# Order of steps in two gate pairs of an encoder block, and the place of the FFN operand's splits

## The chip, the cores and the metric

The kernel runs on one core of a Trainium2 chip. The metric is device time in microseconds (us) from the first to the last instruction of a launch with its overhead, as the median of several runs. The engines of the core work side by side, each on its own list of instructions: TensorE (PE; PEld is its weight load), VectorE (DVE), ScalarE (ACT), GpSimd (POOL) and SyncE (SP), which issues most of the DMAs.

## The reference

One encoder block on 256 tokens of width 2048, all in float32: a projection of the normalised input, three attention mixers, a gated merge of their outputs, an output projection with a residual, and a SwiGLU channel mixer with a residual. What matters here is the part after the mixers:

```python
gates = jax.nn.sigmoid(gt.astype(jnp.float32)).reshape(b, s, N_BRANCH, D_MODEL)
merged = (gates[:, :, 0] * (oa @ w_br_a[layer]).astype(jnp.float32)
          + gates[:, :, 1] * (ob @ w_br_b[layer]).astype(jnp.float32)
          + gates[:, :, 2] * (oc @ w_br_c[layer]).astype(jnp.float32)).astype(x.dtype)
x = x + merged @ w_o[layer]

hf = rms_norm(x, g_ffn[layer]) @ w_ffn_in[layer]
x = x + (jax.nn.silu(hf[..., :D_FF]) * hf[..., D_FF:]) @ w_ffn_out[layer]
```

`gt` are the 6144 gate columns of the first projection, so each gate is a product of the normalised input with a 2048 x 2048 block of weights.

## The kernel before, in words

**Products in halves.** Weights stream from HBM in blocks of 256 rows by 512 columns, held as a tile of 128 x 1024 floats. A float32 product is made of three products of a shorter float format: every operand is written as a high half `hi` plus a low remainder `lo`, and hi·hi, hi·lo and lo·hi are summed in PSUM. For a block of weights, ScalarE copies it to `whi` (L452) and VectorE subtracts that from the block to get `wlo` (L463). For the tokens' side the same is done once for each operand by `split` (L130): ScalarE makes the high half, VectorE the low one. The tokens' side has to lie with its channels on the partitions, so a result of one stage is transposed by TensorE against the identity into a PSUM tile `tp` and then split into the operand of the next stage: `transposed` (L303).

**Pairs and steps.** From the gated merge to the end, the work is a list of *pairs*, each of them two column blocks (c = 0 and c = 1) of 512. `pair` (L465) turns strings of step names into functions. An ordinary step, `d4` or `D4`, is one block of weights for column block 0 or 1: 12 matmuls of 512 columns. The other letters are the seven products with which a 2 x 2 arrangement of blocks is multiplied in place of eight: `X W Y P Z Q H`, each with 6 matmuls. Of them `P`, `Q` and `H` first need a sum or a difference of two weight blocks, which VectorE forms in place (L653, L655, L657) ahead of the split. `S1` to `S4` do the same for a block of one unit: 6 matmuls for each of the first three, two half-size splits, and a half-size sum (L584 to L590). `l0`, `l1`, `r0`, `r1` and `s0` only issue loads. A dot is a free place: it takes the next step of the *tail* of the pair before, that is, ordinary steps that this pair left over.

**What sets the order.** TensorE and SyncE keep the order in which the program was written. On ScalarE and VectorE the order is that of a scheduler with a simulated time line, except for instructions handed to `follow` (L93): each of these is tied behind the last one so handed on its engine, and together they form the sequence of halves. `run` (L690) writes them: it makes a step ready (its in-place sum, if it has one, then its `whi`), then the `wlo` of the step before (`low(1)`), and then emits the products of the step that is four behind (`ahead`), so

```python
            products = ready()
            if products is None:
                continue
            low(1)
            waiting.append(products)
            if len(waiting) > ahead:
                waiting.pop(0)()
                tick()
```

There are five pairs of buffers for `whi` and `wlo` (four in `wp` and, at every fifth step, one in `more`), so a step's `whi` can only be written when the products of the step five before it have been read. What follows a finished column block (sigmoids L975, multiplications L989, additions L995 and L1047, transposes, splits) is written by small side jobs; `tick` lets them go on, and a job that yields n goes on n emitted steps later. These jobs are not in the sequence of halves, but have a high priority with the scheduler.

**Where the change works.** `merging` (L962) runs five gate pairs, numbered by `nth` from 0. Pair 1 takes `STEPS_GATE5` (L57), pair 2 `STEPS_GATE52` (L58). The tail that pair 1 finds is d7, then D0 and d0 of the first branch product; that of pair 2 is d5, d6, d7 of pair 1. In pair 4 the merged block 0 is transposed for the output projection: its job adds the gated products to `mg` (L995), yields 4, and transposes (L1002 to L1006). `projecting` (L1026) makes the output projection in two pairs; each finished block is added to the residual `x` (L1047), squared, transposed and split, scaled by the gain of the FFN's norm, into `x1T` (L1062), the operand of the FFN. In `transposed` a block of 512 columns is done in two halves, each with four transposes and two splits; for `x1T` the second half stood two steps after the first.

Of the kernel before, what the change touches and what calls it, by code (L numbers as in the profile page):

```python
# [11 lines left out]
F32 = mybir.dt.float32  # L12
# [3 lines left out]
ALU = mybir.AluOpType  # L16
# [3 lines left out]
S = 256  # L20
# [33 lines left out]
STEPS_GATE = [  # L54
    ("l0 l1 X0 X1 r0 W0 r1 W1 d4 P0 P1 d5 Y0 Y1 Q0 Q1 Z0 Z1 d6", "D4 H0 D5 H1 D6 D7", "d7"),
    ("l0 l1 X0 X1 . r0 W0 r1 W1 P0 P1 . Y0 Y1 . Q0 Q1 .", "Z0 Z1 D4 H0 D5 H1 D6 D7", "d4 d5 d6 d7")]
STEPS_GATE5 = ("l0 l1 s0 X0 . . X1 S1 r0 W0 r1 W1 P0 P1 S2 . Y0 Y1 Q0 Q1 S3", "Z0 Z1 D5 H0 D6 H1 D7 S4", "d5 d6 d7")  # L57
STEPS_GATE52 = ("l0 l1 s0 X0 . X1 S1 r0 W0 r1 W1 . P0 P1 S2 . Y0 Y1 Q0 Q1 S3",) + STEPS_GATE5[1:]  # L58
STEPS_O = ("l0 s0 X0 S1 . r0 W0 . P0 S2 Y0 . Q0 S3 .", "Z0 D3 H0 D6 S4 d3 D7 d6 D4 D5", "d7 d4 d5")
STEPS_O2 = ("l0 s0 X0 S1 r0 W0 . P0 S2 Y0 . Q0 S3 .", "Z0 D3 H0 D4 S4 d3 D5 D6 D7", "d4 d5 d6 d7")  # L60
STEPS_FFN0 = ("l0 l1 X0 X1 . r0 W0 . r1 W1 . P0 P1 . Y0 Q0 Q1 Y1", "Z0 Z1 D6 H0 D7 H1 D4 D5", "d6 d7 d4 d5")
# [43 lines left out]
def encoder_block(ctx: ExitStack, tc: tile.TileContext, a: dict, out: bass.AP):  # L105
# [21 lines left out]
        return psum.tile([P, NC], F32, name=name, tag=tag, bufs=2 if tag in ("c1", "tp") else 4)  # L127


    def split(hi, lo, src, scale=None):  # L130

        if scale is None:
            nc.scalar.activation(hi, src, AF.Copy)  # L133
            nc.vector.tensor_sub(lo, src, hi.bitcast(F32))  # L134
        else:
            nc.scalar.activation(hi, src, AF.Copy, scale=scale)
            nc.vector.scalar_tensor_tensor(lo, src, scale, hi.bitcast(F32), op0=ALU.mult, op1=ALU.subtract)

    def root_of(v, shape, to):

# [159 lines left out]
            pass  # L300
        known.add(name)

    def transposed(src, dst, g=None, lag=1, also=None, single=None):  # L303


        full = None
        for h in range(2):
            if h:
                yield lag
            tp = bank("tp", "tp")  # L310
            for k in range(2):
                for t in range(T):
                    nc.tensor.transpose(tp[:, k * S + t * P:k * S + (t + 1) * P],
                                        src[t][:, (2 * h + k) * P:(2 * h + k + 1) * P], ident)
            if g is None:
                d = dst(2 * h, 2)
                split(d[0], d[1], tp.rearrange("p (k s) -> p k s", s=S))
            else:
                for k in range(2):
                    d = dst(2 * h + k, 1)  # L320
                    split(d[0], d[1], tp[:, k * S:(k + 1) * S], g(2 * h + k))
            if also is not None:
                if full is None:
                    full = s4([P, 2, 4, P], "ffull")
                to, of = full[:, :, 2 * h:2 * h + 2], tp.rearrange("p (k t s) -> p k t s", t=T, s=P)
                if g is None:
                    nc.scalar.activation(to, of, AF.Copy)
                else:
                    for k in range(2):
                        nc.scalar.activation(to[:, k], of[:, k], AF.Copy, scale=g(2 * h + k))  # L330
            if single is not None and h == 0:
                one = s4([P, 1, 4, P], "ffull")
                nc.scalar.activation(one[:, 0], tp.rearrange("p (k s) -> p k s", s=P), AF.Copy)
                start(urgent(token_sums_later(one, single)))
        if also is not None:
            token_sums(full, also)
# [625 lines left out]
    def merging():  # L962
        nth = 0
        start(lone_of_gates())
        parts = [s8([P, 2, PK, NC], "both", F32, tail) for _ in range(2)]
        extra = [(Part(r[:, i]), f"gate{2 * n + i}") for n, r in enumerate(parts) for i in range(2)]
        free.extend(extra)
        for b, (g0, k0, k1) in enumerate(((0, 0, 2), (8, 2, 6), (4, 6, 12))):
            for j in (0, 2) if b else (2,):
                sg, br = {}, {}  # L970

                def gates(c, r, j=j, b=b, sg=sg, br=br):
                    sg[c] = s4([P, T, NC], "sg")
                    for t in range(T):
                        nc.scalar.activation(sg[c][:, t], r[t], AF.Sigmoid, scale=r_x[:, 0, t:t + 1])  # L975
                    if c in br:
                        merge(c, [br[c][:, t] for t in range(T)], j, b, sg)

                def branch(c, r, j=j, b=b, sg=sg, br=br):
                    if c in sg:  # L980
                        return merge(c, r, j, b, sg)
                    br[c] = s4([P, T, NC], "br")
                    for t in range(T):
                        nc.scalar.activation(br[c][:, t], r[t], AF.Copy)

                def merge(c, r, j, b, sg):
                    n0 = (j + c) * NC
                    for t in range(T):
                        nc.vector.tensor_mul(sg[c][:, t] if b else mg[t][:, n0:n0 + NC], r[t], sg[c][:, t])  # L989

                    def later():
                        yield 1
                        for t in range(T):
                            m = mg[t][:, n0:n0 + NC]
                            nc.vector.tensor_add(m, m, sg[c][:, t])  # L995
                        if b == 2:
                            to = mT[j + c] = s8([P, 2, 4, S], "mT", pool=home(j + c))
                            if j + c == 0:
                                room.extend(form_room(1))
                            if j + c == 1:  # L1000
                                lone["w_o"] = s4([P, 1, 2, 4, P], "lone", F32R)
                            yield 2 if j + c == 2 else 4  # L1002
                            yield from transposed([mg[t][:, n0:n0 + NC] for t in range(T)],
                                                  lambda k, n: (to[:, 0, k:k + n], to[:, 1, k:k + n]),
                                                  lag=2, also=room[0] if j + c == 0 else None,
                                                  single=lone["w_o"] if j + c == 1 else None)  # L1006
                    if b:
                        start(urgent(later()))

                if nth == 3:  # L1010
                    retired.extend(extra)
                    free[:] = [f for f in free if f not in extra]
                front, back, end = pair(block_pair(a["w_gate"], g0 + j), xT,
                                        STEPS_GATE52 if nth == 2 else STEPS_GATE5 if nth == 1 else STEPS_GATE[min(nth, 1)], gates, TWO,
                                        by_room(lambda: gforms), early=nth == 0, fresh="Y" if nth < 2 else "",
                                        single=(4, of_lone("gate")))
                n = (k1 - k0) // 2
                of_br = pair(lambda u, c, j=j, k0=k0: a["w_br"][j + c][k0 // PK + u], lambda k, k0=k0: ol(k0 + k),
                             ("", " ".join(o + str(u) for o in ("dD" if nth else "Dd") for u in range(n)), ""), branch)[1]
                yield (front, back + of_br, end) if nth else (front, back, end + of_br)  # L1020
                nth += 1
# [4 lines left out]
    def projecting():  # L1026
# [16 lines left out]
        for n in (0, 2):  # L1043
            def add(c, r, n=n):
                xc = [x[t][:, (n + c) * NC:(n + c + 1) * NC] for t in range(T)]
                for t in range(T):
                    nc.vector.tensor_add(xc[t], r[t], xc[t])  # L1047
                ended.append(n + c)
                last = len(ended) == 4

                def later():
                    yield 1
                    sq = s4([P, T, NC], "sq")
                    for t in range(T):
                        nc.scalar.activation(sq[:, t], xc[t], AF.Square, accum_out=ss1[:, t, n + c:n + c + 1])
                    if last:
                        start(urgent(root()))
                    yield 2
                    if not x1T:
                        x1T.extend(s8([P, 2, 4, S], "x1T") for _ in range(4))  # L1060
                        room.extend(form_room(3))
                    yield from transposed(xc, lambda k, m: (x1T[n + c][:, 0, k], x1T[n + c][:, 1, k]),  # L1062
                                          lambda k: gT[:, 2, 4 * (n + c) + k:4 * (n + c) + k + 1], 2,
                                          also=room[2 + n + c] if n == 0 else None)
                start(urgent(later()))
            yield pair(block_pair(a["w_o"], n), mTl, STEPS_O2 if n else STEPS_O, add, TWO[:1], by_room(lambda: room),
                       single=(2, of_lone("w_o")))
# [139 lines left out]
```

## Time and profile before

| | |
|---|---|
| median of 3 runs | 1360.47 us (1360.01 to 1360.65) |
| the profiled execution | 1360.15 us, of it 1358.4 us from the first to the last instruction |
| granted TensorE clock | 1.000 |
| TensorE, VectorE, ScalarE busy | 99%, 87%, 64% of the span |
| matmuls and transposes | 6160 |
| moved by DMA | 301.19 MB, 222 GB/s |
| gate pairs 1 and 2 | about 351 to 404 and 404 to 456 us |
| output projection | about 571 to 678 us |

In the time line a row is a run of instructions of one kind: start, duration, engine, line, operation, output and inputs, shape, count, and in brackets the idle time of the engine just before it with what ended it. `raw`, `more` and `both` are the places of loaded weights. `mmX`, `mmW` and so on are the PSUM banks of a pair: X also takes the products `P` and `Q`, W takes `Z` too. `forms` and `glone` are operands of the seven products, `xT`, `oT`, `mT` those of ordinary steps. A busy TensorE isn't TensorE at its peak, since a matmul's end is modelled and overlaps the next one's start: a wait shorter than that overlap shows only in the distance of starts.

### The profile page before, as it was taken

What the parts mean: (1) busy time and instruction counts of PE and PEld (TensorE: products, weight loads), DVE (VectorE), ACT (ScalarE), POOL (GpSimd) and SP (SyncE); (2) the same over time, 40 slices, a digit from 0 to 9 for tenths busy, and PEclk for the clock granted to TensorE, in tenths of its full rate; (3) what the DMA queues carried; (4) which work ended last, traced back from release to release, by engine and by line L of the source; (5) the groups of instructions that cost most, each with busy time, mean ns of one, the idle gap of its engine ahead of it and who ended that gap; (6) DMA issues with size and microseconds to landing.
All of it is one profiled execution on the core that took longest, in us unless ns stands there. A gap on an engine that the chain in (4) does not pass through costs nothing.

```text
span 1358.4 us, 17355 instructions
## 1 busy us (share of the span) xinstructions
PE 1350.5 (99%) x6160; PEld 1118.3 (82%) x6160; DVE 1176.4 (87%) x1458; ACT 864.4 (64%) x1136; POOL 53.1 (4%) x60
## 2 busy tenths in 40 slices
PE   9999999999999999999999999999999999999998
PEld 8888888888887888888888888888888888888887
DVE  6878877768989869788999998988999889989997
ACT  7876665655666656656776666555666655566664
POOL 0010000000000000000000000000000000000000
PEclk9999999999999999999999999999999999999999
DMA  9976455558494594873678666688666786666872
GB/s 368 348 240 210 141 155 181 160 162 288 186 307 144 184 297 154 287 253 118 224 233 263 209 205 215 225 263 262 191 216 215 248 263 209 219 221 210 277 223 98
DMA packets 86344, 301.19 MB, mean 222 GB/s; under 512 B 9777, under 2 KB 12337, under 8 KB 86001
## 3 DMA queue, kind: packets, MB, share of 16 engines
q1 hardware_dynamic: 79488, 275.94, 57.8%
q0 software_dynamic: 6624, 24.12, 9.4%
q8 instruction: 48, 0.79, 0.2%
q14 instruction: 40, 0.32, 0.1%
q10 hardware_dynamic: 144, 0.02, 0.0%
HBM read 297.17 MB, written 2.88 MB: 221 GB/s over the span
## 4 chain that ended last, share of the span: by engine, by line
PE 95%; DVE 3%; ACT 1%; issue 1%; POOL 0%; DVEq 0%; POOLq 0%; ACTq 0%
PE mmX L80 28%; PE mmW L80 20%; PE mm L80 17%; PE mmY L80 15%; PE mmQ L80 11%; DVE wlo L463 2%; PE tp L80 1%; PE sc L80 1%; PE o L80 1%; PE pT L80 1%; PE mmV L80 1%; PE hT L80 0%; ACT whi L452 0%; PE idle L80 0%; DVE both L655 0%
## 5 line engine op out<-in xcount | busy, mean ns | idle before, releaser
L452 ACT ACTIVATE whi<-raw 128x1024 fp32r<-128x1024 f32 (+1 forms) x354 | 360.8, 1036 | 214.7 <-DVE raw L657 49.9
L463 DVE TENSOR_TENSOR wlo<-raw,whi 128x1024 fp32r<-128x1024 f32 (+1 forms) x354 | 418.0, 1195 | 64.6 <-ACT whi L452 61.0
L80 PE MATMUL mm<-whi,xT 128*128 128x512 f32 x640 | 202.9, 393 | 0.0
L452 ACT ACTIVATE whi<-both 128x1024 fp32r<-128x1024 f32 (+1 forms) x117 | 117.9, 1015 | 66.8 <-PE mmQ L80 22.1
L463 DVE TENSOR_TENSOR wlo<-both,whi 128x1024 fp32r<-128x1024 f32 (+1 forms) x117 | 136.1, 1169 | 24.9 <-ACT whi L452 24.5
L134 DVE TENSOR_TENSOR wlo<-raw,whi 128x1024 fp32r<-128x1024 f32 x82 | 104.2, 1274 | 42.9 <-ACT whi L133 40.6
L452 ACT ACTIVATE whi<-more 128x1024 fp32r<-128x1024 f32 (+1 forms) x103 | 106.7, 1037 | 54.4 <-DVE more L655 18.1
L80 PEld LDWEIGHTS mm<-whi,xT 128*128 128x128 f32 x640 | 119.2, 188 | 24.2 <-issue 1.1
L463 DVE TENSOR_TENSOR wlo<-more,whi 128x1024 fp32r<-128x1024 f32 (+1 forms) x103 | 123.2, 1198 | 14.6 <-ACT whi L452 14.0
L133 ACT ACTIVATE whi<-raw 128x1024 fp32r<-128x1024 f32 x82 | 87.0, 1062 | 66.3 <-PE mm L80 51.7
L80 PE MATMUL mm<-wlo,xT 128*128 128x512 f32 x320 | 125.5, 392 | 0.0
L80 PE MATMUL mmW<-whi,forms 128*128 128x512 f32 x368 | 122.1, 390 | 0.0
L80 PE MATMUL mmX<-whi,forms 128*128 128x512 f32 x368 | 122.0, 390 | 0.0
L80 PE MATMUL mmX<-whi,x1T 128*128 128x512 f32 x352 | 120.9, 389 | 0.0
L80 PE MATMUL mmY<-whi,x1T 128*128 128x512 f32 x264 | 89.1, 389 | 0.0
L80 PEld LDWEIGHTS mmW<-whi,forms 128*128 128x128 f32 x368 | 69.1, 188 | 14.3
L80 PEld LDWEIGHTS mmX<-whi,forms 128*128 128x128 f32 x368 | 69.1, 188 | 14.2
L80 PEld LDWEIGHTS mmX<-whi,x1T 128*128 128x128 f32 x352 | 66.1, 188 | 13.7
L80 PE MATMUL mmX<-wlo,forms 128*128 128x512 f32 x184 | 71.8, 390 | 0.2 <-DVE wlo L463 0.2
L80 PE MATMUL mmW<-wlo,forms 128*128 128x512 f32 x184 | 71.7, 390 | 0.2 <-DVE wlo L463 0.2
L80 PEld LDWEIGHTS mm<-wlo,xT 128*128 128x128 f32 x320 | 60.2, 188 | 11.6
L80 PE MATMUL mmX<-wlo,x1T 128*128 128x512 f32 x176 | 68.5, 389 | 0.0
(311 smaller groups left out, 2606.4 us busy)
## 6 DMA issues: line engine op xcount, KB each, us to landing
raw<-in_w_ffn SPq DMA_DIRECT2D x109, 512.0 KB, 8.0
raw<-in_w_qkv SPq DMA_DIRECT2D x64, 512.0 KB, 4.3
raw<-in_w_gate SPq DMA_DIRECT2D x58, 512.0 KB, 5.0
raw<-in_w_ffn_out SPq DMA_DIRECT2D x53, 512.0 KB, 7.4
both<-in_w_ffn SPq DMA_DIRECT2D x34, 512.0 KB, 6.5
more<-in_w_ffn SPq DMA_DIRECT2D x33, 512.0 KB, 6.9
both<-in_w_gate SPq DMA_DIRECT2D x24, 512.0 KB, 8.9
raw<-in_w_o SPq DMA_DIRECT2D x24, 512.0 KB, 6.0
```

The costliest lines, as they stand in the source:

```text
L80: ins = op(*args, **kw)
L133: nc.scalar.activation(hi, src, AF.Copy)
L134: nc.vector.tensor_sub(lo, src, hi.bitcast(F32))
L452: nc.follow(nc.scalar.activation(hi[:, o], v, AF.Copy))
L463: nc.follow(nc.vector.tensor_sub(*part))
```

## The change

There are three edits. In the string of pair 1 the third dot moves from behind `S2` to a place behind `W0`, ahead of `r1 W1`. In that of pair 2 the second dot moves from behind `W1` to one behind `X1`, ahead of `S1`, and the third from behind `S2` to one behind `W0`, ahead of `r1 W1`. The transposes of merged block 0 start 5 steps after the job's additions in place of 4. For `x1T`, the splits of a half are written one step after its transposes and are handed to `follow`, so they stand in the sequence of halves; the second half still comes two steps after the first.

```diff
-STEPS_GATE5 = ("l0 l1 s0 X0 . . X1 S1 r0 W0 r1 W1 P0 P1 S2 . Y0 Y1 Q0 Q1 S3", "Z0 Z1 D5 H0 D6 H1 D7 S4", "d5 d6 d7")
-STEPS_GATE52 = ("l0 l1 s0 X0 . X1 S1 r0 W0 r1 W1 . P0 P1 S2 . Y0 Y1 Q0 Q1 S3",) + STEPS_GATE5[1:]
+STEPS_GATE5 = ("l0 l1 s0 X0 . . X1 S1 r0 W0 . r1 W1 P0 P1 S2 Y0 Y1 Q0 Q1 S3", "Z0 Z1 D5 H0 D6 H1 D7 S4", "d5 d6 d7")
+STEPS_GATE52 = ("l0 l1 s0 X0 . X1 . S1 r0 W0 . r1 W1 P0 P1 S2 Y0 Y1 Q0 Q1 S3",) + STEPS_GATE5[1:]
...
-    def split(hi, lo, src, scale=None):
+    def split(hi, lo, src, scale=None, put=lambda ins: ins):
...
-            nc.scalar.activation(hi, src, AF.Copy, scale=scale)
-            nc.vector.scalar_tensor_tensor(lo, src, scale, hi.bitcast(F32), op0=ALU.mult, op1=ALU.subtract)
+            put(nc.scalar.activation(hi, src, AF.Copy, scale=scale))
+            put(nc.vector.scalar_tensor_tensor(lo, src, scale, hi.bitcast(F32), op0=ALU.mult, op1=ALU.subtract))
...
-    def transposed(src, dst, g=None, lag=1, also=None, single=None):
+    def transposed(src, dst, g=None, lag=1, also=None, single=None, chain=False):
...
+            if chain:
+                yield 1
...
-                    split(d[0], d[1], tp[:, k * S:(k + 1) * S], g(2 * h + k))
+                    split(d[0], d[1], tp[:, k * S:(k + 1) * S], g(2 * h + k), *[nc.follow] * chain)
...
-                            yield 2 if j + c == 2 else 4
+                            yield {0: 5, 2: 2}.get(j + c, 4)
...
-                                          lambda k: gT[:, 2, 4 * (n + c) + k:4 * (n + c) + k + 1], 2,
-                                          also=room[2 + n + c] if n == 0 else None)
+                                          lambda k: gT[:, 2, 4 * (n + c) + k:4 * (n + c) + k + 1], 1,
+                                          also=room[2 + n + c] if n == 0 else None, chain=True)
```

More of the change, by code (lines that the diff above doesn't have):

```diff
@@ L127, in bank @@
         return psum.tile([P, NC], F32, name=name, tag=tag, bufs=2 if tag in ("c1", "tp") else 4)
-    def split(hi, lo, src, scale=None):
+    def split(hi, lo, src, scale=None, put=lambda ins: ins):
         if scale is None:
-            nc.scalar.activation(hi, src, AF.Copy)
-            nc.vector.tensor_sub(lo, src, hi.bitcast(F32))
-        else:
-            nc.scalar.activation(hi, src, AF.Copy, scale=scale)
-            nc.vector.scalar_tensor_tensor(lo, src, scale, hi.bitcast(F32), op0=ALU.mult, op1=ALU.subtract)
+            put(nc.scalar.activation(hi, src, AF.Copy))
+            put(nc.vector.tensor_sub(lo, src, hi.bitcast(F32)))
+        else:
+            put(nc.scalar.activation(hi, src, AF.Copy, scale=scale))
+            put(nc.vector.scalar_tensor_tensor(lo, src, scale, hi.bitcast(F32), op0=ALU.mult, op1=ALU.subtract))
     def root_of(v, shape, to):
```

## The prediction

> **What bounds the kernel now.** I read the page first, then the time line of each engine around every place where TensorE's matmuls start further apart than elsewhere, then what was queued on VectorE and ScalarE there.
>
> ```profile
> PE 1350.5 (99%) x6160; PEld 1118.3 (82%) x6160; DVE 1176.4 (87%) x1458; ACT 864.4 (64%) x1136; POOL 53.1 (4%) x60
> ```
>
> TensorE is the bound, and the change takes no matmul away. So all it can win are the places where TensorE waits. The chain of waits shows what an undisturbed stretch looks like:
>
> ```profile
> 967.71 4.08 PE mmX L80 x18
> ```
>
> That is 4.08 / 18 = 0.227 us from start to start. One matmul is shown as 0.39 long, so a wait of 0.16 is hidden under its end. TensorE's time line at the waits near the edits:
>
> ```profile
> 375.46 0.50 PE L80 MATMUL mmX<-wlo,forms 128*128 128x512 f32 x1 [0.23 <-DVE wlo L463]
> ...
> 381.20 0.50 PE L80 MATMUL mmW<-wlo,xT 128*128 128x512 f32 x1
> ...
> 430.06 0.50 PE L80 MATMUL mmW<-wlo,forms 128*128 128x512 f32 x1 [0.17 <-DVE wlo L463]
> ...
> 433.47 0.50 PE L80 MATMUL mmW<-wlo,xT 128*128 128x512 f32 x1 [0.37 <-DVE wlo L463]
> ...
> 542.79 0.27 PE L80 MATMUL tp<-ident,mg 128*128 128x128 f32 x1
> 543.87 0.55 PE L80 MATMUL tp<-ident,mg 128*128 128x128 f32 x3 [0.81 <-DVE mg L995]
> ...
> 629.71 0.50 PE L80 MATMUL mmY<-wlo,mT 128*128 128x512 f32 x1 [0.71 <-DVE wlo L463]
> ```
>
> Each row with a bracket lost the idle time shown, the 0.16 hidden ahead of it, and 0.11 because the released matmul is 0.50 long in place of 0.39. This gives four places. **A** (pair 1): Q1 0.50 and D5, which has no bracket but the long matmul, 0.16 + 0.11 = 0.27 at most, together 0.77. **B** (pair 2): Z0 0.44 and D5 0.64, together 1.08. **C** (transposes of merged block 0 in pair 4): 1.08 from the first to the second, where the three after it stand (0.55 - 0.27) / 2 = 0.14 apart, so 0.94. **D** (ordinary step d4 in the second output pair): 0.98. In all 3.77 us, 0.28% of the time. No outcome can be much better than this.
>
> **Edit 1, the dots.** In A and B the `wlo` of VectorE comes last. How much room VectorE has there:
>
> ```profile
> 354.00:382.00 28.00, 27.34 (x31) 1.00 0.26 88
> 398.00:434.00 36.00, 34.63 (x40) 1.00 0.53 193
> ```
>
> (Window, its length, VectorE's busy time, granted clock, DMA share.) In A it stands idle for 0.66 of 28 us, in B for 1.37 of 36. The edit removes and adds no VectorE work ahead of the late halves, Q1 and D5 in A, Z0 and D5 in B; it only orders it anew. So it can win at most these holes, and it loses whatever new holes it makes. Therefore I follow the holes. A, VectorE:
>
> ```profile
> 354.40 1.23 DVE L463 TENSOR_TENSOR wlo<-more,whi 128x1024 fp32r<-128x1024 f32 x1 [0.17 <-ACT whi L452]
> 355.66 1.23 DVE L653 TENSOR_TENSOR more<-more,raw 128x1024 f32<-128x1024 f32 x1
> 357.13 0.69 DVE L989 TENSOR_TENSOR mg<-mmW,sg 128x512 f32<-128x512 f32 x1 [0.24 <-PE mmW L80]
> 357.74 1.22 DVE L463 TENSOR_TENSOR wlo<-raw,whi 128x1024 fp32r<-128x1024 f32 x1
> 358.88 0.68 DVE L989 TENSOR_TENSOR mg<-mmQ,sg 128x512 f32<-128x512 f32 x1
> 359.48 1.22 DVE L653 TENSOR_TENSOR raw<-raw,both 128x1024 f32<-128x1024 f32 x1
> ...
> 366.11 1.23 DVE L463 TENSOR_TENSOR wlo<-raw,whi 128x1024 fp32r<-128x1024 f32 x1 [0.20 <-ACT whi L452]
> ```
>
> and ScalarE beside it:
>
> ```profile
> 356.36 1.05 ACT L452 ACTIVATE whi<-raw 128x1024 fp32r<-128x1024 f32 x1
> ...
> 358.54 1.06 ACT L452 ACTIVATE whi<-more 128x1024 fp32r<-128x1024 f32 x1 [1.13 <-PE mmQ L80]
> ```
>
> By starts a 1024-wide operation takes 1.14 (357.74 to 358.88), a 512-wide one 0.61. The rows are, in order: W0's `wlo`, P0's sum (L653), a merge, W1's `wlo`, a merge, P1's sum. The `whi` at 356.36 is W1's and waits for a buffer: the one that d7, five steps before, gives back. P0's, at 358.54, waits in the same way for D0's products. With the dot behind W0, d0 stands where W1 stood: its `whi` comes at 356.36, and W1's at 358.54. P0's sum needs no buffer, and today it fills the time in which VectorE would wait for the `whi` of 356.36. In the new sequence the `wlo` of d0 must come ahead of P0's sum (`low(1)` after W1 is made ready), so the sum can't fill that hole: VectorE has nothing from 355.54 to 357.13, does the merge, d0's `wlo` and a merge, and only then P0's sum, at 359.48 in place of P1's. From there on one operation of 1.14 us more is left to do ahead of Q1. The hole of 0.28 (0.20 shown) at 366.11, Y0's wait for its `whi`, goes, because VectorE comes there late; d0's early merge is work that was ahead of Q1 already. A loses 1.14 - 0.28 = 0.86. Queued behind the late `wlo` on VectorE are S3, Z0, Z1, the sum of H0 and D5's `wlo`, without a hole today, so the delay reaches D5 undiminished; TensorE waits for it.
>
> B is the same with d7 ahead of W1, and d6 ahead of S1:
>
> ```profile
> 415.83 1.22 DVE L463 TENSOR_TENSOR wlo<-more,whi 128x1024 fp32r<-128x1024 f32 x1 [0.40 <-ACT whi L452]
> 417.16 1.23 DVE L463 TENSOR_TENSOR wlo<-both,whi 128x1024 fp32r<-128x1024 f32 x1
> ```
>
> ```profile
> 407.90 1.06 ACT L452 ACTIVATE whi<-both 128x1024 fp32r<-128x1024 f32 x1 [1.66 <-PE mmX L80]
> ```
>
> The `whi` at 407.90 is d6's, released by d5. In its place stands d7's, whose `wlo` can't start before 408.96; P0's sum, which today fills the time ahead of d6's `wlo`, must follow it. At 409 the sequence has done W1's `wlo` and P0's sum less and d6's `wlo` more: 1.14 behind. Later it saves the holes of 0.40 at 415.83 and 417.16 - 415.83 - 1.14 = 0.19 at 417.16. A new wait, Y0's `whi` for d7's products, is covered by d7's merges (4 of 0.61), which then come early; without that cover it would cost up to 0.9 (estimated from the starts). B loses 1.14 - 0.59 = 0.55. Bounds: from the holes won back, -0.66 and -1.08 (B can't win more than it waits), to a full 1.14 each plus the uncovered 0.9 in B.
>
> These losses hold if a waiting instruction really keeps back those behind it; the rows under D show that it does on ScalarE (2.54 us). [...]
>
> The moved steps' loads change place on SyncE's queue too:
>
> ```profile
> 392.46 0.33 SPq L80 DMA_DIRECT2D more<-in_w_gate  x1
> ```
>
> ```profile
> both<-in_w_gate SPq DMA_DIRECT2D x24, 512.0 KB, 8.9
> ```
>
> This is d7's load in B. It goes ahead of the two loads of r1, the last of which then leaves at this time and lands about 8.9 later, at 401.4; its first reader, P1's sum, comes after 409. In A d0's load goes ahead of r1's in the same way, and no wait shown above, in A or B, is ended by a DMA. d0, d6 and d7 are loaded earlier than today by two issues or more, and GpSimd's additive loads (of l0 and l1) stand ahead of all of this. Cost nothing, hidden by some 8 us between landing and use; a landing later than that would hold up P1's sum.
>
> **Edit 2, the transposes of merged block 0.**
>
> ```profile
> 542.00 1.22 DVE L463 TENSOR_TENSOR wlo<-raw,whi 128x1024 fp32r<-128x1024 f32 x1
> ```
>
> The transposes wait for the second addition L995, done when they go on at 543.87. A step later they come behind D5 (12 matmuls, 2.72 us), at 545.5, and find it done. Next late is D5's own `wlo`, the row above: it ends at 543.22, while its first reader would start at 542.79 + 0.23 = 543.02. That is 0.20 and some latency, 0.25. C wins 0.94 - 0.25 = 0.69; bounds 0.4 (the addition scheduled still later) and 0.94. The operand made from it, `mT`, is first read by the output projection, from about 571: covered by over 20 us.
>
> **Edit 3, the splits into `x1T`.** ScalarE, then VectorE, ahead of D:
>
> ```profile
> 620.76 1.04 ACT L452 ACTIVATE whi<-both 128x1024 fp32r<-128x1024 f32 x1
> ...
> 624.71 0.84 ACT L136 ACTIVATE x1T<-tp,gT 128x256 fp32r<-128x256 f32 x2 [2.54 <-PE tp L80]
> ...
> 627.33 2.01 ACT L452 ACTIVATE whi<-raw 128x1024 fp32r<-128x1024 f32 x2
> ```
>
> ```profile
> 628.43 1.23 DVE L463 TENSOR_TENSOR wlo<-raw,whi 128x1024 fp32r<-128x1024 f32 x1 [1.71 <-ACT whi L452]
> ```
>
> The scheduler put splits on ScalarE ahead of d4's `whi`; they wait 2.54 us for transposes, `whi` comes at 627.33, `wlo` ends at 629.66, and TensorE waits. In the sequence, the first half's splits stand behind Y0's `whi` (620.76) and the second half's behind Q0's, each after its transposes. d4's `whi` then comes at about 621.7 + 0.84 = 622.5, its `wlo` behind Y0's and Q0's sum at about 626.5, over 2 us ahead of need. D wins its 0.98. In return four small VectorE operations of a block join the sequence, each after a ScalarE operation of 0.42: some tenths, covered by those 2 us. Bounds: -0.98, or +1 if a block of the other three takes on such a wait.
>
> **Sum.** 0.86 + 0.55 - 0.69 - 0.98 = -0.26 us. Against the profiled execution's 1360.15 us that is 1359.9; the median of the runs lies 0.32 above it, so **1360.2 us**: edits 2 and 3 win about 1.7 us, edit 1 gives most of it back. A measurement of this kernel can tell about 0.2% from no change, 2.7 us.
>
> **Rivals.** *All four waits go.* If VectorE finds other work for the two holes (the scheduler may place the free merges there), A and B vanish and D5 in C isn't late: -3.77, 1356.7 us. For it: an ordinary step holds its buffer for 2.72 us of TensorE in place of 1.36, so more products lie ready when the costly sums begin. Against it: VectorE is 98% and 96% busy there, and the merges become ready too late for the first hole. Chance 0.24; I count here all cases that win over 2.7.
>
> *The chained splits block the sequence* (slower). ScalarE works splits and halves in one line; if in the other three blocks of `x1T` a split waits for its transposes as at 624.71, each costs TensorE what D shows, 0.98, and D's own stays: 0.86 + 0.55 - 0.69 + 3 x 0.98 = +3.7, 1364.1 us. It decides from the point at which a split waits longer than the 2 us that the halves are ahead. For it: the order is now fixed. Against it: a step lies between transposes and splits. Chance 0.09.
>
> *The edits don't reach what they aim at*: the scheduler moves the addition L995 with the transposes, and another free instruction blocks ScalarE ahead of d4. Then C and D stay: +1.41, 1361.9 us. Against it: L995 is written before the yield that grows. Chance 0.09.
>
> **Chances.** The forecast has 0.58; it and the third rival lie within 0.2%: 0.67. Faster 0.24, slower 0.09. The forecast's bounds run from a few tenths lost in edit 1 (-1.7, 1358.8) to both sums lost in full (+0.9, 1361.4); the range reaches down to the first rival and up to the third: 1356.7 to 1362.0.
>
> **What would show it.** Right: in pair 1 VectorE idle for over 1 us just ahead of the merge at 357.13; Q1 and D5 together late by about 1.6 us in A and in B; no wait of `tp` for L995; d4's `wlo` over 1 us ahead of its matmul; no idle time on ScalarE ahead of the `x1T` splits. Wrong: A and B without waits, or a wait for a `wlo` in the output projection with L137 just ahead of it.

## The result, and the profile after

The changed kernel takes **1364.78 us** (median of 7 runs, 1364.34 to 1365.35) where the kernel before takes 1360.47 (7 runs, 1359.59 to 1360.89): a ratio of 1.0033, 95% interval 1.0021 to 1.0044. It is 4.31 us slower; the forecast was 1360.2 us, and the time lies above the range. The profiled execution, 1364.78 us itself, has a span of 1363.0 us, 4.6 more than before, at a granted clock of 0.999.

The page, the busy time of each engine and the chain that ended last:

```profile
PE 1351.4 (99%) x6160; PEld 1117.3 (82%) x6160; DVE 1177.4 (86%) x1458; ACT 864.9 (63%) x1136; POOL 53.1 (4%) x60
...
PE 89%; DVE 7%; ACT 2%; issue 1%; DMA 0%; SPq 0%; DVEq 0%; ACTq 0%
```

The same chain in the kernel before, where VectorE has 3% of it in place of 7%:

```profile
PE 95%; DVE 3%; ACT 1%; issue 1%; POOL 0%; DVEq 0%; POOLq 0%; ACTq 0%
```

The work is the same: the same number of instructions on each engine, and TensorE's busy time differs by 0.9 us. The place where it stands still is another. The two lines of TensorE's waits that are new:

```profile
PE mmX L80 <- DVE mmW L629: 4.0, 4, 1.2
PE mmW L80 <- DVE wlo L465: 1.9, 2, 1.1
```

(From `transposed` on the changed kernel is two lines longer: its L465 is L463 of before, L629 is L627, L991 is L989; L136 and L137 are the two operations of `split`. The kernels below are shifted by a few lines in the same way.) The waits for L995 and for `mmY` are gone. The wait in the first row is one that the kernel before did not have: L629 forms a product sum, `W = m5 - X`, from bank X at the end of the `P` products, and the products of `Q` are written into that bank, so Q0 must wait until L629 has read it. TensorE's time line has these places one by one:

```profile
374.70 0.47 PE L80 MATMUL mmX<-whi,forms 128*128 128x512 f32 x1 [1.15 <-DVE mmW L629]
...
427.57 0.47 PE L80 MATMUL mmX<-whi,forms 128*128 128x512 f32 x1 [1.17 <-DVE mmW L629]
...
544.30 0.39 PE L80 MATMUL mmW<-whi,xT 128*128 128x512 f32 x1
544.78 0.50 PE L80 MATMUL mmW<-wlo,xT 128*128 128x512 f32 x1
...
632.88 0.47 PE L80 MATMUL mmX<-whi,forms 128*128 128x512 f32 x1 [0.53 <-DVE mmW L629]
...
681.88 0.47 PE L80 MATMUL mmX<-whi,forms 128*128 128x512 f32 x1 [1.18 <-DVE mmW L629]
...
691.20 0.50 PE L80 MATMUL mmW<-wlo,x1T 128*128 128x512 f32 x1 [1.07 <-DVE wlo L465]
...
696.36 0.50 PE L80 MATMUL mmW<-wlo,x1T 128*128 128x512 f32 x1 [0.78 <-DVE wlo L465]
```

The first two are in gate pairs 1 and 2, 544.30 is D5 of pair 4, 632.88 lies in the second output pair. The last three stand in the first stretch of the FFN, where TensorE lost almost nothing before; they are most of the loss.

To compare kernels I sum, for each stretch, the distance from each matmul's start to the next less the undisturbed one (the median in the trace of before: 0.227 us for 512 columns, 0.120 for 256, 0.109 for a transpose). This holds also the waits that hide under a matmul's modelled end, which lies 0.39 us behind its start at 512 columns. Each row is from the one profiled execution of its kernel. A and B are the two pairs (340 to 404, 404 to 456 us), C is 456 to 571, D the output projection (571 to 650), E its end and the start of the FFN (650 to 705):

| us lost by TensorE | A | B | C | D | E |
|---|---|---|---|---|---|
| before | 0.76 | 1.21 | 1.35 | 1.28 | 0.11 |
| changed | 1.75 | 1.79 | 0.73 | 1.11 | 4.04 |
| difference | +0.99 | +0.58 | -0.62 | -0.17 | +3.93 |
| by the prediction | +0.86 | +0.55 | -0.69 | -0.98 | 0 |

The differences come to +4.7, the span's to +4.6.

### The profile page after: what moved, and what is told of

Its sections match the earlier page's. It is cut to its first block, busy times and chain, and to the rows that moved or that the text cites. A ratio compares the mean times of both kernels' runs of the same rounds, so it can differ in the third digit from the quotient of the medians.

```text
span 1363.0 us, 17360 instructions
## 1 busy us (share of the span) xinstructions
PE 1351.4 (99%) x6160; PEld 1117.3 (82%) x6160; DVE 1177.4 (86%) x1458; ACT 864.9 (63%) x1136; POOL 53.1 (4%) x60
## 4 chain that ended last, share of the span: by engine, by line
PE 89%; DVE 7%; ACT 2%; issue 1%; DMA 0%; SPq 0%; DVEq 0%; ACTq 0%
PE mmX L80 26%; PE mmW L80 19%; PE mm L80 17%; PE mmY L80 13%; PE mmQ L80 10%; DVE wlo L465 4%; PE tp L80 1%; PE sc L80 1%; PE o L80 1%; ACT whi L454 1%; PE pT L80 1%; DVE raw L657 0%; PE mmV L80 0%; DMA raw<-in_w_mem 0%; PE hT L80 0%
## 5 line engine op out<-in xcount | busy, mean ns | idle before, releaser
L465 DVE TENSOR_TENSOR wlo<-raw,whi 128x1024 fp32r<-128x1024 f32 (+1 forms) x361 | 422.1, 1185 | 72.5 <-ACT whi L454 69.6
L454 ACT ACTIVATE whi<-both 128x1024 fp32r<-128x1024 f32 (+1 forms) x109 | 112.7, 1040 | 54.5 <-DVE both L657 12.2
L465 DVE TENSOR_TENSOR wlo<-both,whi 128x1024 fp32r<-128x1024 f32 (+1 forms) x109 | 130.3, 1200 | 14.7 <-ACT whi L454 13.5
L465 DVE TENSOR_TENSOR wlo<-more,whi 128x1024 fp32r<-128x1024 f32 (+1 forms) x104 | 124.1, 1199 | 12.4 <-ACT whi L454 11.7
```

The lines of the kernel that those rows point to most:

```text
L454: nc.follow(nc.scalar.activation(hi[:, o], v, AF.Copy))
L465: nc.follow(nc.vector.tensor_sub(*part))
```

## The experiments

All times are medians of 6 to 11 runs (4 for the fifth kernel), each with the median of the kernel before that was run beside it, and in brackets the ratio with its 95% interval. Where that interval holds 1, the times alone show no difference; there the account rests on the losses by stretch. After the result I held that the loss in A and B comes from VectorE's work there, an idle place that nothing fills (H in the expectations), against a rival that Q0's new wait comes from where L629 stands (S); and that the loss in D and E comes from the splits' place in the sequence, against the step's delay or the transposes.

**Each edit alone.** The first kernel has only the two strings, the second only the transposes' step, the third only the `x1T` part:

```diff
+STEPS_GATE5 = ("l0 l1 s0 X0 . . X1 S1 r0 W0 . r1 W1 P0 P1 S2 Y0 Y1 Q0 Q1 S3", "Z0 Z1 D5 H0 D6 H1 D7 S4", "d5 d6 d7")
+STEPS_GATE52 = ("l0 l1 s0 X0 . X1 . S1 r0 W0 . r1 W1 P0 P1 S2 Y0 Y1 Q0 Q1 S3",) + STEPS_GATE5[1:]
```

> The kernel before with edit 1 alone (the dots of pairs 1 and 2 moved). Theory H (holes of VectorE): P0's sum loses the hole it filled, so A and B lose what the changed kernel's trace shows against before, about 1.0 and 0.6 us: 1.5 us slower than before, and TensorE waits first at Q0. Rival S (the subtraction L627, which reads bank X and now stands behind Q1's sum, is what is late): the same time here; e8 tells the two apart. If edits 1 and 3 only hurt together, under 0.5 us slower.

```diff
-                            yield 2 if j + c == 2 else 4
+                            yield {0: 5, 2: 2}.get(j + c, 4)
```

> The kernel before with edit 2 alone (merged block 0 transposed a step later). All theories: the wait of the transposes for L995 goes, D5's low half is late by about 0.25 us: 0.7 us faster than before. If the addition moves with the transposes: no difference.

```diff
+            if chain:
+                yield 1
...
+                    split(d[0], d[1], tp[:, k * S:(k + 1) * S], g(2 * h + k), *[nc.follow] * chain)
```

> The kernel before with edit 3 alone (splits of x1T a step later and in the sequence of halves). Theory C (the sequence is blocked by splits in which the second high half waits for the first remainder): about 4.3 - 1.5 + 0.7 = 3.5 us slower than before, lost in the last block of x1T at the start of the FFN. Rival E (edit 1 makes VectorE late and edit 3 only suffers from it): under 1 us slower.

Measured, beside 1360.25: the strings 1361.94 (ratio 1.0013, 1.0004 to 1.0023), the transposes' step 1359.55 (0.9997, 0.9988 to 1.0007), the splits 1364.25 (1.0032, 1.002 to 1.0045). The three differences, +1.69, -0.70 and +4.00, add up to +4.99, beside +4.31 for all three. By stretch each edit does its own part: the strings have A 1.75 and B 1.80, the step C 0.74, the splits D 1.09 and E 4.06; all else is as before to within 0.2. So edit 1 loses about what was forecast, and what lies beyond the forecast is edit 3's.

**The delay without the sequence.** The third kernel, but the splits are left to the scheduler:

```diff
-                    split(d[0], d[1], tp[:, k * S:(k + 1) * S], g(2 * h + k), *[nc.follow] * chain)
+                    split(d[0], d[1], tp[:, k * S:(k + 1) * S], g(2 * h + k))
```

> The kernel before with the splits of x1T written a step later but not handed to follow. Theory C: the sequence isn't blocked, so within 1 us of before, and the wait of d4 in the second output pair may go. Rival L (the step's delay itself makes the operand late): as slow as e3, about 3.5 us.

1359.07 (0.9993, 0.9983 to 1.0002); D falls from 1.28 to 0.27, and E stays at 0.11. ScalarE's time line in this kernel, ahead of d4's matmuls:

```profile
620.87 1.04 ACT L454 ACTIVATE whi<-both 128x1024 fp32r<-128x1024 f32 x1
621.81 0.45 ACT L136 ACTIVATE x1T<-tp,gT 128x256 fp32r<-128x256 f32 x1
...
622.65 1.05 ACT L454 ACTIVATE whi<-raw 128x1024 fp32r<-128x1024 f32 x1
```

One split of the first half goes ahead of d4's `whi`, without a wait, and `whi` comes at 622.65 in place of 627.33. So the gain of edit 3 is all in the delay; the place in the sequence loses 5.2 us against it.

**The sequence without the delay.** Against the third kernel:

```diff
-            if chain:
-                yield 1
...
-                                          lambda k: gT[:, 2, 4 * (n + c) + k:4 * (n + c) + k + 1], 1,
+                                          lambda k: gT[:, 2, 4 * (n + c) + k:4 * (n + c) + k + 1], 2,
```

> The kernel before with the x1T splits in the sequence of halves, but written at once with the transposes, not a step later. Theory C (the place in the sequence costs, the delay doesn't): as slow as with the delay or slower, 4 us or more above before, since ScalarE then also waits for the transposes themselves. Rival L (sequence and delay only hurt together): under 1 us above before.

1366.39, beside 1360.22 (1.0047, 1.0032 to 1.0062); D 2.23, E 4.90. Without the delay the kernel stands 6.17 above before, with it 4.00: in the sequence the delay is worth 2.2 us. The expectation's reason, that ScalarE then also waits for the transposes, does not show. All waits of the `x1T` splits on ScalarE from 600 to 700 us, in this kernel and in the changed one:

```profile
ACT x1T L136 <- DVE x1T L137: 5.0, 8, 1.2
```

```profile
ACT x1T L136 <- DVE x1T L137: 6.4, 8, 1.9
```

There are eight halves of a block in this stretch, and with the delay or without it ScalarE waits once in each, for VectorE and never for a transpose. What the 2.2 us are made of stays open.

**What the sequence waits for.** ScalarE in the changed kernel, around 688 us, and VectorE beside it:

```profile
685.49 0.45 ACT L136 ACTIVATE x1T<-tp,gT 128x256 fp32r<-128x256 f32 x1
687.88 0.47 ACT L136 ACTIVATE x1T<-tp,gT 128x256 fp32r<-128x256 f32 x1 [1.94 <-DVE x1T L137]
690.12 1.06 ACT L454 ACTIVATE whi<-more 128x1024 fp32r<-128x1024 f32 x1 [1.77 <-DVE more L659]
```

```profile
687.37 0.48 DVE L137 SCALAR_TENSOR_TENSOR x1T<-tp,gT,x1T 128x256 fp32r<-128x256 f32 x1
688.39 0.48 DVE L137 SCALAR_TENSOR_TENSOR x1T<-tp,gT,x1T 128x256 fp32r<-128x256 f32 x1 [0.54 <-ACT x1T L136]
688.79 1.22 DVE L659 TENSOR_TENSOR more<-raw,more 128x1024 f32<-128x1024 f32 x1
```

A half of a block has two splits, of the two column tiles k = 0 and 1, and they were written hi0, lo0, hi1, lo1. hi0 (ScalarE) is done at 685.94. hi1 needs nothing that VectorE makes; it starts at 687.88 all the same, right after lo0 (VectorE) ends at 687.85. Meanwhile VectorE stands idle for 0.54, for lo1 is next in its sequence and waits for hi1; the sum L659, behind lo1 in that sequence, starts at 688.79, and the next `whi`, which waits for the sum, at 690.12. The two engines hand the turn to each other. The bracket at 687.88 is read from a semaphore of VectorE that the instruction waits for, so the turn is an order that stands in the program. How much VectorE loses shows in its waits from 660 to 698 us, in the changed kernel:

```profile
DVE x1T L137 <- ACT x1T L136: 3.6, 6, 1.0
```

and in the windows view (length, VectorE's busy time, its instructions, clock, DMA share, GB/s) of before, of the changed kernel and of the one with the delay alone:

```profile
660.00:700.00 40.00, 38.81 (x56) 1.00 0.64 194
```

```profile
660.00:700.00 40.00, 35.43 (x46) 1.00 0.61 182
```

```profile
660.00:700.00 40.00, 38.82 (x55) 1.00 0.68 209
```

VectorE is 97% busy there before, so the 3.4 us that it loses can't be made up: L629 and the `wlo` of this stretch come late, at 681.88, 691.20 and 696.36. Two kernels, each the third with one thing changed, separate the turns from the place: in the first, both high halves are written ahead of both low ones; in the second, the column tiles lie in two PSUM banks in place of one.

```diff
+                to = [dst(2 * h + k, 1) for k in range(2)]
+                put = nc.follow if chain else lambda ins: ins
                 for k in range(2):
-                    d = dst(2 * h + k, 1)
-                    split(d[0], d[1], tp[:, k * S:(k + 1) * S], g(2 * h + k), *[nc.follow] * chain)
+                    put(nc.scalar.activation(to[k][0], tp[:, k * S:(k + 1) * S], AF.Copy, scale=g(2 * h + k)))
+                for k in range(2):
+                    put(nc.vector.scalar_tensor_tensor(to[k][1], tp[:, k * S:(k + 1) * S], g(2 * h + k),
+                                                       to[k][0].bitcast(F32), op0=ALU.mult, op1=ALU.subtract))
```

> As e3 (edit 3 alone), but within a half of a block both high halves are written ahead of both remainders. Theory P (the second high half waits 0.54 us for the first remainder each time, and that idles VectorE and holds ScalarE): the loss of 4.0 us falls to 2 us or less, to 1362.3 or below. Rival Q (what costs is the place alone: high halves behind a whi that waits for a sum, remainders ahead of the next sum): still over 3 us slower than before.

1361.34, beside 1360.22 (1.0007, 0.9998 to 1.0016): 2.9 less than the third kernel stood above its own runs of before. E falls from 4.06 to 1.63, D from 1.09 to 0.58. VectorE's waits from 660 to 698 us in this kernel:

```profile
DVE x1T L326 <- ACT x1T L324: 2.8, 3, 1.5
```

The second wait of each half is gone; the first, for hi0, remains and is longer at its longest. I read it as coming from the place: hi0 stands behind a `whi` that itself waits for a sum of VectorE, and ScalarE shows the same kind of wait as at 690.12 above, 3.19 us, for a sum (L663) at 686.71. That the sequence causes what remains is shown by the last kernel below, which has the high halves first and the delay but no sequence, with edit 2, which shows in C alone (D 0.27, E 0.11); which place in it does so was not tested by itself.

```diff
-            tp = bank("tp", "tp")
+            tps = [bank("tp", "tp") for _ in range(1 + chain)]
+            tp, at = tps[0], lambda k: tps[k][:, :S] if chain else tps[0][:, k * S:(k + 1) * S]
...
-                    split(d[0], d[1], tp[:, k * S:(k + 1) * S], g(2 * h + k), *[nc.follow] * chain)
+                    split(d[0], d[1], at(k), g(2 * h + k), *[nc.follow] * chain)
...
```

> As e3 (edit 3 alone), but the two column tiles of a half are transposed into two PSUM banks in place of one. Theory K (the second high half waits for the first remainder because both read one bank): the waits of 0.55 us on ScalarE for L137 go, and the time is like that with the high halves first, about 1361.3, unless TensorE waits for the banks. Rival (the order comes from the gain or the x1T tile): the waits stay, 1364.2.

The order as written is that of the third kernel, hi0, lo0, hi1, lo1. ScalarE's time line and TensorE's waits in this kernel:

```profile
623.74 0.82 ACT L136 ACTIVATE x1T<-tp,gT 128x256 fp32r<-128x256 f32 x2
```

```profile
PE tp L80 <- ACT ffull L333: 1.5, 1, 1.5
...
PE tp L80 <- DVE x1T L137: 0.5, 1, 0.5
```

hi0 and hi1 now run without a gap, so it is the shared bank that makes the turns (a bank is one tile in these kernels, so the two can't be told apart here). E falls to 1.04. But a half now takes both `tp` banks, the next transposes wait for the readers of them, and D rises from 1.09 to 2.63. B rises to 2.60 as well, with a gate load that arrives later (ScalarE waits 4.63 us for it, to 399.62, where before it waited 2.72, to 397.52) and that the edit does not touch; this execution, 1364.01 us, is the slowest of the ten, 1.3 above their median. The whole: 1362.67 (1361.98 to 1364.01), beside 1360.64, a ratio of 1.0015 (1.0006 to 1.0024).

With one bank hi1 starts 0.03 us after lo0's end (687.85 to 687.88 in the changed kernel, 624.02 to 624.05 in the half ahead of D), with two right behind hi0 (0.82 for both). What two such reads would do without the wait between them no run here shows.

**Highs first in the kernel before**, without delay or sequence:

```diff
+                to = [dst(2 * h + k, 1) for k in range(2)]
                 for k in range(2):
-                    d = dst(2 * h + k, 1)
-                    split(d[0], d[1], tp[:, k * S:(k + 1) * S], g(2 * h + k))
+                    (nc.scalar.activation(to[k][0], tp[:, k * S:(k + 1) * S], AF.Copy, scale=g(2 * h + k)))
+                for k in range(2):
+                    (nc.vector.scalar_tensor_tensor(to[k][1], tp[:, k * S:(k + 1) * S], g(2 * h + k),
+                                                       to[k][0].bitcast(F32), op0=ALU.mult, op1=ALU.subtract))
```

> The kernel before, splits where they were and free for the scheduler, but both high halves of a half ahead of both remainders, in all three operands that are split with a scale. If the 2.54 us on ScalarE ahead of d4 were a wait for the first remainder (L137 ends at 624.58), they go and with them 1.0 us of TensorE's time: 1359.3. If they were a wait for the transposes, as the row says: no difference, 1360.3.

1359.79, beside 1360.22 (0.9997, 0.9987 to 1.0006). D falls from 1.28 to 0.60, but ScalarE's wait ahead of D stays:

```profile
624.82 0.84 ACT L321 ACTIVATE x1T<-tp,gT 128x256 fp32r<-128x256 f32 x2 [2.16 <-PE tp L80]
```

The 2.54 us that the prediction quoted were for the transposes, as it read them; only 0.4 of them came from the turns.

**The strings: what Q0 waits for.** In the first kernel Q0 waits for the subtraction (L627 there) and not for a `wlo`. This kernel takes that subtraction out of the sequence, so that the scheduler may put it earlier:

```diff
-                    nc.follow(nc.vector.tensor_sub(ps["W"], raws["m5"], ps["X"]))
+                    nc.vector.tensor_sub(ps["W"], raws["m5"], ps["X"])
```

> Edit 1 alone, with the subtraction L627 at the end of the P products not handed to follow, so that it can run as soon as its products are done. Theory H (holes): VectorE has the same work ahead of D5, so A and B stay about 1.0 and 0.6 us worse than before, 1361.7, and TensorE waits for a wlo in place of the subtraction. Rival S: the loss goes, under 0.5 us slower than before.

1360.93, beside 1360.22 (1.0005, 0.9996 to 1.0015). Its waits on TensorE at these places:

```profile
PE mmX L80 <- DVE wlo L463: 1.1, 2, 0.6
```

The wait for the subtraction is gone, and a `wlo` is late in its place: A 1.72 and B 1.77 stay as they were in the first kernel (1.75 and 1.80). The rival falls; it is the amount of VectorE's work ahead of Q0. It stands only 0.71 above before, and the first one 1.69. In the profiled executions that lies for the most part in other stretches: against the first one C is 0.45 lower and the part ahead of 340 us 0.2 lower.

The last test of the strings gives VectorE back what filled the idle place: P0's sum is written when W1 is made ready.

```diff
-                if kind == "P":
+                if sum_first and kind == "W" and m == 1:
+                    nc.follow(nc.vector.tensor_add(raws[0]["t"], raws[0]["t"], raws[0]["b22"]))
+                if kind == "P" and not (sum_first and m == 0):
...
```

> Edit 1 alone, but P0's sum is written when W1 is made ready, so it stands on VectorE ahead of the wlo of the step before W1 and can fill the hole again. Theory H: the losses go; A and B hold no more wait than before (0.76 and 1.21 us by distance of starts), and up to the late holes of 0.28 and 0.59 less: 1359.4 to 1360.3. Rival S (the subtraction L627 still stands behind Q1's sum and is late for Q0 by itself): A and B stay at 1.75 and 1.80.

1360.76, beside 1360.64 (1.0003, 0.9993 to 1.0012). VectorE in the changed kernel, and in this one:

```profile
354.32 1.23 DVE L465 TENSOR_TENSOR wlo<-more,whi 128x1024 fp32r<-128x1024 f32 x1 [0.18 <-ACT whi L454]
357.05 0.69 DVE L991 TENSOR_TENSOR mg<-mmW,sg 128x512 f32<-128x512 f32 x1 [1.50 <-PE mmW L80]
357.66 1.22 DVE L465 TENSOR_TENSOR wlo<-both,whi 128x1024 fp32r<-128x1024 f32 x1
358.79 1.22 DVE L655 TENSOR_TENSOR more<-more,raw 128x1024 f32<-128x1024 f32 x1
```

```profile
354.07 1.23 DVE L463 TENSOR_TENSOR wlo<-more,whi 128x1024 fp32r<-128x1024 f32 x1 [0.18 <-ACT whi L452]
355.33 1.23 DVE L653 TENSOR_TENSOR more<-more,raw 128x1024 f32<-128x1024 f32 x1
356.80 0.69 DVE L991 TENSOR_TENSOR mg<-mmW,sg 128x512 f32<-128x512 f32 x1 [0.24 <-PE mmW L80]
```

With the sum in it the hole of 1.50 shrinks to 0.24, and A is back at 0.79: in A, the lost filler is the whole of edit 1's cost. B only falls from 1.80 to 1.55. I take it that S1's half-size sum, which the dot ahead of it now also holds back, makes up the rest; this was not tried.

**The best version.** Edit 2 and the delay of edit 3, with the strings and the splits' freedom as before; and the same with the high halves first:

> Edit 2 and the later x1T splits without the sequence (e2 and e4 together), dots as before. Additive: 0.7 + 1.2 = 1.9 us faster than before, 1358.3. If the scheduler places other work worse: between 1358.3 and 1360.

> As e11, and both high halves of a half ahead of both remainders in every split with a scale. The waits around x1T are gone already in e11, so no difference to e11: 1358.3, within 0.4.

1358.59 and 1358.74, beside 1360.64: ratios 0.9984 (0.9976 to 0.9993) and 0.9985 (0.9976 to 0.9993). All that TensorE still waits for in the first of the two, beside the start of the program:

```profile
PE mmW L80 <- DVE wlo L465: 0.6, 2, 0.4
PE mmX L80 <- DVE wlo L465: 0.2, 1, 0.2
```

C is 0.73 and D 0.27, the two gains next to each other. The high halves first bring nothing once the splits come a step later. This version beats both kernels: the one before by 0.16%, and its median is 6.2 us below that of the changed one, whose runs were not taken beside these.

## Why the prediction was wrong, point by point

**Edit 1: the size held, the place of the wait did not.** +1.57 by stretch and +1.69 by the time, forecast 1.41. The hole ahead of the merge at 357.05 is there (1.50, "over 1 us"), P0's sum comes after it, and in A giving it back undoes the loss. That a waiting instruction keeps back those behind it the prediction had shown on ScalarE alone (2.54 us); on VectorE this hole shows it, with P0's sum left standing behind the merge until 358.79, an operation that in the kernel with the sum moved ran at 355.33. But the lateness was to show at the `wlo` of Q1 and D5 (A) and of Z0 and D5 (B). It shows at Q0, at 374.70 and 427.57. I had followed only the late halves, and not that `Q` writes a bank which VectorE must have read. VectorE is behind by the same amount whichever of its results is asked for first, so the sum held. The first rival, that the scheduler finds other work for the holes, is refuted by that hole of 1.50.

**Edit 2: right.** C -0.62, forecast -0.69. The wait of `tp` for L995 is gone, and D5's `wlo` is late in its place: 544.30 to 544.78 is 0.48, and less the 0.227 it is 0.25, the figure of the prediction.

**Edit 3: here the forecast failed**, at the step "In return four small VectorE operations of a block join the sequence, each after a ScalarE operation of 0.42: some tenths, covered by those 2 us." Its first part was right: no split waits for transposes, d4's matmul waits for nothing (there is no wait for `mmY`). Three things were not so.

The price of joining was counted as the operations' own length, hi and then lo, while the rows hold a chain: hi0, lo0, hi1, lo1, each after the other. One such turn stood in the trace of the kernel before, a ScalarE split held until VectorE's had ended:

```profile
625.73 0.47 ACT L136 ACTIVATE x1T<-tp,gT 128x256 fp32r<-128x256 f32 x1 [0.19 <-DVE x1T L137]
```

From 600 to 700 us of the changed kernel VectorE loses 0.54 for hi1 in each of the eight halves and in four of them also a wait for hi0, in all 8.1 us in 12 waits; and the sign "no idle time on ScalarE ahead of the `x1T` splits" failed eight times. Ahead of D:

```profile
623.54 0.48 DVE L137 SCALAR_TENSOR_TENSOR x1T<-tp,gT,x1T 128x256 fp32r<-128x256 f32 x1 [1.92 <-ACT x1T L136]
624.56 0.48 DVE L137 SCALAR_TENSOR_TENSOR x1T<-tp,gT,x1T 128x256 fp32r<-128x256 f32 x1 [0.54 <-ACT x1T L136]
...
627.23 1.22 DVE L465 TENSOR_TENSOR wlo<-both,whi 128x1024 fp32r<-128x1024 f32 x1
...
632.05 0.69 DVE L629 TENSOR_TENSOR mmW<-m,mmX 128x512 f32<-128x512 f32 x1
```

That is 2.46 in one half in place of "some tenths".

The cover was counted once and at d4. d4's `wlo`, at 627.23 (its block lies in `both` here), came in time for its matmul; the forecast was about 626.5. What stands behind it in the sequence, L629, ended at 632.74, and Q0 waits 0.53 for it at 632.88. So D won 0.17 in place of 0.98.

And the bound, "+1 if a block of the other three takes on such a wait", was sized by the wait at D. In E VectorE was 97% busy before, so there was no cover at all, and E lost 3.93. The row that would have told it, VectorE's busy time from 660 to 700 us, does not stand in the prediction, which has that view for A and B alone.

**The rivals.** *The chained splits block the sequence* (chance 0.09, 1364.1 us) had the sign and, from terms that were not the ones, nearly the size (1364.78 was measured). Its mechanism was three blocks waiting for their transposes at 0.98 each. Shown is another: the turns at a shared bank (2.9 of the third kernel's 4.0, by the kernel with the highs first), and the sequence itself for what remains, as I read it by the place behind a `whi` that waits for a sum. What it had in common with the truth is that a fixed order makes each of two engines wait for the other; it deserved more than 0.09, as the rows under D had shown what one blocked line costs. *The edits don't reach what they aim at* is refuted: edit 2 reached L995, edit 3 d4.

## What to carry to other kernels

Before an instruction is tied into a fixed order on two busy engines, write down for each engine what stands right behind it, and what it waits for on the other one; a pair that read one PSUM bank in turn cost each engine here about the length of the other's operation (0.54 and 0.55 us for operations of 0.47 and 0.48), so write all of one engine's reads first (2.9 us less lost here). Check the cover where the instruction will run, from the busy share of that stretch, not where the gain is. When a step is moved ahead of a filler (an operation that needs no buffer), reckon the filler's length, less the holes that close behind it, as the price (here 0.86 and 0.55 us, measured 0.99 and 0.58); it appeared here at the dependent that was asked for first, Q0 (waits of 1.15 and 1.17).

## What the runs showed of the hardware

In the changed kernel two engines that only read one PSUM bank, in different columns, did not overlap: in each of the eight halves ScalarE's second 128x256 read started 0.03 us after VectorE's first had ended (687.85 to 687.88), and with two banks the two ScalarE reads took 0.82 together. What holds the second read is, by the profile, a wait for the other engine's semaphore, so the rows show an order in the program and its price; what the chip would do without it no run shows. On VectorE each such hand-over was a hole of 0.54 to 0.55 us; writing the high halves first took 2.9 us off TensorE's loss in D and E (5.15 to 2.21).
